# A different start for the first 128 columns of some low weight parts in a two-layer decoder trunk

## The chip, the core and the metric

The kernel runs on one core of a Trainium2 chip. The metric is device time in microseconds (us), from one launch to its end. Three timed runs of the kernel before the change took 2015.96, 2016.24 and 2016.65 us; the median is 2016.24 us.

The core's engines work side by side: TensorE (PE) multiplies matrices, and its weight loads (PEld) are recorded apart; VectorE (DVE) does elementwise work, ScalarE (ACT) copies and activation functions, GpSimd (POOL) and SyncE (SP) start most of the transfers.

## The reference

Two layers over 256 tokens of width 2048, in float32. Layer 0 has full causal attention over its one block of 256 tokens, layer 1 has sliding-window attention (window 128) with shared keys and values and a sink for each head. Both are followed by a gated feed-forward net of width 5504 with a causal convolution of three taps. After each part there is a residual and a layer norm.

```
def conv_ffn(x, w_up, conv_w, conv_b, w_down):
    h = x @ w_up                       # 2048 -> 2 * 5504
    ...                                # causal depthwise convolution, width 3
    g, v = jnp.split(hc, 2, axis=-1)
    return (jax.nn.gelu(g) * v) @ w_down

for layer in range(DEPTH):             # DEPTH = 2
    attn = moba_attention(...) if layer < N_A_LAYERS else swa_attention(...)
    h = layer_norm(ALPHA * h + attn, ln_g[layer, 0], ln_b[layer, 0])
    ffn = conv_ffn(h, ffn_w_up[layer], ffn_conv_w[layer], ffn_conv_b[layer], ffn_w_down[layer])
    h = layer_norm(ALPHA * h + ffn, ln_g[layer, 1], ln_b[layer, 1])
```

Nearly all the time goes into products of 256 tokens with large weight matrices, which are each read once from memory.

## The kernel before

**Two parts for each number.** The multiplier works on a rounded form of float32 (`F32R`). To keep accuracy, each weight `raw` is split into a high part `wh` (a rounded copy, made by ACT, L194) and a low part `wl` = `raw` - `wh` (made by DVE, L203). The activations are split in the same way: `xT` holds, for each of 16 blocks of 128 features, 256 columns of high parts and behind them 256 columns of low parts. A product is the sum of high weight times high activation, high weight times low activation, and low weight times high activation.

**Halves.** Weights stream through in pieces of 128 x 1024 floats, called halves here (`HW = 1024`). Half `s` is loaded by SP into one of 7 `raw` buffers, then split into one of 4 `wh` and one of 4 `wl` buffers. `split_upto` keeps the splits some halves ahead of the use; after each low part it issues the next load.

**Where weights stand still.** In the products for queries, keys and the feed-forward up-projection, a block of 128 x 128 weights is loaded into the multiplier (PEld) and the activations move past it. One unit is 128 output features: two halves, 16 blocks of weights. For each block `k` there is one *high matmul* (weights from `wh`, all 512 columns of `xT[:, k]`: L364, L391) and one *low matmul* (weights from `wl`, the 256 high columns: L367, L391). In the row `L391 PE MATMUL acc<-xT,wl`, `acc` is the accumulator, `xT` the moving operand and `wl` the weights. High matmuls that follow each other are called a high row here, low matmuls that follow each other a low row.

- `ws_unit` (all 52 units of queries and keys, and units 4 to 11 of each up-projection): 8 high, 16 low, 8 high matmuls. Matmuls of attention may be put in after the first half, which cuts the 16 low ones into 8 and 8, or after the second.
- `ws_turns` (units 12 to 85 of each up-projection): 16 high then 16 low in even units, 16 low then 16 high in odd ones. Across units this makes high rows and low rows of 32.
- `ws_opening` (units 0 to 3 of each up-projection): the high matmuls of four units in two passes of 256 columns each (L413), then the low matmuls of the four units (L425) as one row of 64. Units 0 and 1 have `wl` buffers; units 2 and 3 lie in other tiles (`up` in the trace).

In all other products (values, output and down projections) the activations stand still and the weights move.

**The shift.** A `wl` buffer is 64 floats longer than a half (`PAD = 64`). For halves whose weights stand still, the low part is written 48 floats (192 bytes) behind the buffer's first byte (`SHIFT = 48`); for all others, and for halves that lie in other tiles, it starts at the first byte. `wh` always starts at the first byte. In the built program `xT` and all `wh` and `wl` buffers start at the same remainder of 256 bytes, and a block of 128 floats is 512 bytes, so an address differs in this remainder from the others only by the shift.

**Order.** The order on each engine is written out by hand. `next_halves` makes the list of halves with their shifts; `high_upto` takes the buffers; `low_piece` writes the low part; `cols(w, j)` gives the j-th block of 128 columns of a half to a matmul. In the up-projection DVE also does the convolution (L1323 to L1334), and SP and POOL start transfers between places in device memory that sum weights for later (`t<-in_wq_dram`, `t<-t`).

Of the kernel before, what the change touches and what calls it, by code (L numbers as in the profile page):

```python
# [12 lines left out]
F32 = mybir.dt.float32  # L13
F32R = mybir.dt.float32r
AF = mybir.ActivationFunctionType
ALU = mybir.AluOpType
AX = mybir.AxisListType

P = 128
T = 256  # L20
D = 2048
# [4 lines left out]
DFF = 5504  # L26
# [16 lines left out]
HW = 1024  # L43
SHIFT = 48
PAD = 64
# [9 lines left out]
OPENING = 4  # L55
TURNS = 12
# [25 lines left out]
def quad_halves(l, n):  # L82

    if n >= 2:
        return wo_halves(QUADS[l][n])
    q = QUADS[l][n]
    plain = [(k, c) for c in range(2) for k in range(2 * q, FT)]  # L90
    two = lambda *b: ("w", *b, *(plain.pop(0) for _ in range(2 - len(b))))
    order = [two() for _ in range(LEAD[l][n])]
    tight = max(q - (len(plain) - (n * 2 * (DOWN_WINDOW[l] + TRAIL[l]) or 6)) // 2, 0)
    for i, j in enumerate(j for j in TWO_QUADS[l][n] if 2 * j < q):
        for x in range(2):
            a, b = (4 * j + 2 * x, 0), (4 * j + 2 * x + 1, 0)
            sums = [("t", j, 2 * x), ("t", j, 2 * x + 1)]
            if i < tight - (0 if x else q // 2):
                order += [sums[0], two(a, b), sums[1]]
            else:  # L100
                order += [sums[0], two(a), sums[1], two(b)]
        order.append(two((4 * j + 1, 1), (4 * j + 3, 1)))
    return order + [two() for _ in range(len(plain) // 2)]


def wo_halves(q):


    halves = lambda bs: [("w", *bs[i:i + 2]) for i in range(0, len(bs), 2)]
    if q == 6:  # L110
        order = halves([(2 * p + 1, c) for c in range(2) for p in range(q)] + [(12, 0), (13, 0)])
        for i, j in enumerate((2, 0, 1)):
            t = [("t", j, x) for x in range(4)]
            order += t[:2] + halves([(4 * j, 0), (4 * j + 2, 0)]) + t[2:] + (halves(WO_MID) if i == 0 else [])
        return order + halves(WO_LAST)
    q = range(q)
    mid = [b for p in q for b in ((2 * p, 0), (2 * p + 1, 0), (2 * p + 1, 1))]
    mid[5:5] = WO_MID[:1]
    mid[10:10] = WO_MID[1:]
    order = halves(WO_LEAD)  # L120
    sums, others = [("t", j, i) for j in range(len(q) // 2) for i in range(4)], halves(mid)
    while sums:
        order += [sums.pop(0)] + others[:1]
        others = others[1:]
    return order + others + halves(WO_LAST)
# [7 lines left out]
def trunk(ctx: ExitStack, tc: tile.TileContext, wst, wq, xT_in, x_in, relb, umask, sinks, conv_in, ln_g, ln_b, out):  # L133
    nc = tc.nc
# [5 lines left out]
    spool = ctx.enter_context(tc.tile_pool(name="spool", bufs=HALF_BUFS))  # L140
# [4 lines left out]
    tsum = {q: dram.tile([4, P, HW], F32, name=f"t{i}") for i, q in enumerate(QUAD_LIST)}  # L145
    source, used = [], iter(range(wst.shape[0]))

    def next_halves(width, shift=0):
        return [(wst[next(used)], shift) for _ in range(width * D // (P * HW))]

    def next_quads(l, n):
        return [(tsum[l, n, h[1]][h[2]] if h[0] == "t" else wst[next(used)], 0) for h in quad_halves(l, n)]

    for l, width in enumerate((D, KVH * P)):
        if QUADS[l][3]:
            source += next_halves(D // 2) + next_halves(D, SHIFT) + next_quads(l, 3) + next_halves(D, SHIFT)
        else:
            source += next_halves(width) + next_halves((2 * D, KVH * P + D)[l], SHIFT)
        source += next_quads(l, 2) + next_halves(D // 2) if QUADS[l][2] else next_halves(D)
        source += next_halves(2 * DFF, SHIFT) + next_quads(l, 0) + next_quads(l, 1)  # L160
    source, shifts = zip(*source)
    n_halves = len(source)
    raws, halves, aside = {}, {}, {}
# [3 lines left out]
    def pieces(u):  # L167
        return (slice(0, HW // 2), slice(HW // 2, HW)) if u < RAW_FIRST else (slice(0, HW),)
# [11 lines left out]
    def home(tile, j):  # L180

        return [tile[:, k:k + 2, :].rearrange("p a b -> p (a b)") for k in (4 * j, 4 * j + 2)]

    def high_upto(i, behind=None):
        while todo["high"] <= min(i, n_halves - 1):
            s = todo["high"]
            if s in aside:
                wh, wl = home(*aside.pop(s))
            else:
                wh = spool.tile([P, HW], F32R, name="wh")  # L190
                wl = spool.tile([P, HW + PAD], F32R, name="wl")[:, shifts[s]:shifts[s] + HW]
            halves[s] = placed[s] = (wh, wl)
            for j, c in enumerate(pieces(s)):
                nc.scalar.activation(wh[:, c], raws[s][:, c], AF.Copy)  # L194
                if len(pieces(s)) > 1:
                    low_piece(s, c)
                if behind:
                    behind(j)
            todo["high"] += 1

    def low_piece(s, c):
        wh, wl = placed[s]
        nc.vector.tensor_tensor(out=wl[:, c], in0=raws[s][:, c], in1=wh[:, c].bitcast(F32), op=ALU.subtract)  # L203

    def split_upto(i, behind=None):
        while todo["low"] <= min(i, n_halves - 1):
            s = todo["low"]
            high_upto(s, behind)
            if len(pieces(s)) == 1:
                low_piece(s, slice(0, HW))  # L210
            placed.pop(s)
            raws.pop(s)
            load_weights()
            todo["low"] += 1
# [28 lines left out]
    def take(ahead=AHEAD):  # L243
        i = nexth["i"]
        nexth["i"] += 1
        run(ahead_of_splits)
        if i in reach:
            run(before)
        upto = max(i + ahead, reach.get(i, 0))
        if between_splits:  # L250
            high_upto(upto)
            between_splits.pop()()
        split_upto(upto)
        run(before)
        return halves.pop(i)
# [49 lines left out]
    for i, (name, w) in enumerate((("nm", 2), ("rsm", 2), ("sm", 2), ("es", 2), ("ag", 2), ("sd", 1), ("rs", 1))):  # L305
        o = 8 * i - 4 * (name == "rs")
# [46 lines left out]
        nc.vector.scalar_tensor_tensor(b, b, 1 / SCALE, mask.to_broadcast([P, h1 - h0, 2 * P]), op0=ALU.mult, op1=ALU.add)  # L353

    def cols(w, j):
        return w[:, j * P:(j + 1) * P]

    def ws_unit(acc):


        o = acc[:, 0:T]

        def high(wh, k, j, stop=False):
            nc.tensor.matmul(acc, cols(wh, j), xT[:, k, :], start=(k == 0), stop=stop)  # L364

        def low(wl, k, j):
            nc.tensor.matmul(o, cols(wl, j), xT[:, k, 0:T], start=False, stop=False)  # L367

        wh, wl = take()
        for j in range(8):  # L370
            high(wh, j, j)
        for j in range(8):
            low(wl, j, j)
        step()
        wh, wl = take()
        for j in range(8):
            low(wl, 8 + j, j)
        for j in range(8):
            high(wh, 8 + j, j, stop=(j == 7))
        step()  # L380

    def ws_turns(acc, low_first):


        i = nexth["i"]
        pair = [take(AHEAD - 1), take(AHEAD - 2)]

        def row(n, first):
            o, moving = (acc[:, 0:T], slice(0, T)) if n else (acc, slice(0, 2 * T))
            for k in range(KB):  # L390
                nc.tensor.matmul(o, cols(pair[k // 8][n], k % 8), xT[:, k, moving], start=(first and k == 0),  # L391
                                 stop=(not first and k == KB - 1), skip_group_check=True)

        row(int(low_first), True)
        step()
        split_upto(i + 1 + AHEAD)
        run(before)
        row(int(not low_first), False)
        step()
# [224 lines left out]
    def project_out(src, nk, li, homes, preload, turnover=None, work=None, early_sums=None, wo_sums=None, src_pair=None, last_place=None, row_place=None, up=None, direct=None, held=()):  # L624
# [227 lines left out]
        def late(t, i):  # L852
# [15 lines left out]
            if t == 1 and after:  # L868
                first = 3 if work is None else window - 4
                if first <= i < first + 4:  # L870
                    c = COLS[0][i - first]
                    low(0, c, turn(0, c))
                if 5 <= i < 7:
                    high_upto(n0 + i + 1)
# [662 lines left out]
```

## Time and profile before

| | |
|---|---|
| median of three runs | 2016.24 us (2015.96 to 2016.65) |
| the profiled execution | 2015.96 us |
| span from its first to its last instruction | 2014.0 us |
| layer 0: attention with its output projection | up to about 372 us |
| layer 0: up-projection, then down-projection | about 372 to 855, then to 1110 us |
| layer 1: attention with its output projection | up to about 1310 us |
| layer 1: up-projection, then down-projection | about 1310 to 1791, then to 2014 us |

In rows of the timeline the columns are: start, time from the start of the first to the end of the last instruction, engine, line, operation, names, shapes, count. Matmuls are pipelined, and the end that is recorded for one lies beyond the start of the next. So the pace of a row is read from start to start: the start of the next row less the start of this one, divided by the count; or, inside one row, the time of the row less the recorded duration of one matmul, divided by the count less one.

### The profile page before, as it was taken

Reading aid. Unit: us, or ns where it says so; the run is one execution under the profiler, and the core shown is the slowest. Engines: PE = TensorE matmul, PEld = TensorE weight load, DVE = VectorE, ACT = ScalarE, POOL = GpSimd, SP = SyncE. Lnnn points to the kernel's source line nnn. Section 1 sums busy time; section 2 is a strip of 40 time slices with the busy share of each in tenths; the row PEclk is TensorE's granted clock in tenths of the full one; section 3 lists DMA queues with packets and bytes.
Section 4 is the critical chain, followed back from the end, with each engine's and each line's share of the span. In section 5 each row is a group of like instructions: output and inputs, shape, how many; then the busy total and the mean of one; then the engine's idle time right before and its main releaser. Section 6 shows DMA issues by size and latency. Waiting matters only on the chain.

```text
span 2014.0 us, 30061 instructions
## 1 busy us (share of the span) xinstructions
PE 2005.6 (100%) x10894; PEld 1740.1 (86%) x10894; DVE 1699.2 (84%) x2573; ACT 1151.8 (57%) x1648; POOL 130.7 (6%) x177
## 2 busy tenths in 40 slices
PE   9999999999999999999999999999999999999998
PEld 8888888988888888888888888898888888888886
DVE  6878789798888888799997788988888887889988
ACT  5557566345455544477774678545445454467674
POOL 0000000011011010000001000010100011000000
PEclk9999999999999999999999999999999999999999
DMA  9999989899999999589998979989999999769895
GB/s 364 315 265 323 359 257 346 277 329 348 319 333 341 318 345 313 196 301 371 346 396 244 294 240 294 362 239 347 321 323 315 322 324 328 247 197 365 330 366 213
DMA packets 149172, 626.07 MB, mean 311 GB/s; under 512 B 19902, under 2 KB 21310, under 8 KB 136288
## 3 DMA queue, kind: packets, MB, share of 16 engines
q1 hardware_dynamic: 135312, 539.44, 70.7%
q0 software_dynamic: 13424, 84.47, 21.5%
q8 instruction: 85, 1.39, 0.3%
q14 instruction: 63, 0.52, 0.1%
q10 hardware_dynamic: 288, 0.26, 0.0%
HBM read 621.95 MB, written 165.71 MB: 391 GB/s over the span
## 4 chain that ended last, share of the span: by engine, by line
PE 98%; DVE 1%; DMA 0%; ACT 0%; issue 0%; ACTq 0%; DVEq 0%
PE acc L391 41%; PE acc L364 12%; PE acc L367 6%; PE acc L607 5%; PE acc L606 5%; PE acc L605 5%; PE at L607 3%; PE at L606 3%; PE at L605 3%; PE acc L1109 2%; PE acc L450 2%; PE acc L449 2%; PE acc L448 2%; PE acc L413 2%; PE at L967 1%; PE acc L425 1%
## 5 line engine op out<-in xcount | busy, mean ns | idle before, releaser
L203 DVE TENSOR_TENSOR wl<-raw,wh 128x1024 fp32r<-128x1024 f32 (+1 forms) x782 | 944.3, 1215 | 185.8 <-ACT wh L194 112.1
L194 ACT ACTIVATE wh<-raw 128x1024 fp32r<-128x1024 f32 (+1 forms) x782 | 821.8, 1053 | 432.5 <-issue 207.6
L391 PE MATMUL acc<-xT,wh 128*128 128x512 f32 x2368 | 552.5, 391 | 0.0
L391 PEld LDWEIGHTS acc<-xT,wh 128*128 128x128 f32 x2368 | 439.4, 188 | 89.9
L391 PEld LDWEIGHTS acc<-xT,wl 128*128 128x128 f32 x2368 | 289.3, 188 | 5.6
L391 PE MATMUL acc<-xT,wl 128*128 128x256 f32 x2368 | 290.8, 280 | 0.0
L364 PE MATMUL acc<-xT,wh 128*128 128x512 f32 x1088 | 261.6, 392 | 0.0
L364 PEld LDWEIGHTS acc<-xT,wh 128*128 128x128 f32 x1088 | 199.5, 188 | 39.9
L1322 ACT ACTIVATE work<-acc 128x256 f32<-128x256 f32 x172 | 65.6, 382 | 186.0 <-PE acc L391 177.7
L367 PEld LDWEIGHTS acc<-xT,wl 128*128 128x128 f32 x1088 | 139.5, 188 | 5.2
L367 PE MATMUL acc<-xT,wl 128*128 128x256 f32 x1088 | 143.6, 280 | 0.0
L324 POOL DMA_DIRECT2D t<-in_wq_dram x78 | 61.7, 791 | 940.3 <-DMA t<-in_wq_dram 931.1
L324 POOL DMA_DIRECT2D t<-t x78 | 61.0, 781 | 603.6 <-DMA t<-in_wq_dram 422.1
L1325 DVE SCALAR_TENSOR_TENSOR work<-work,cw,work 128x255 f32<-128x255 f32 x172 | 83.2, 484 | 6.1
L1326 DVE SCALAR_TENSOR_TENSOR work<-work,cw,work 128x254 f32<-128x254 f32 x172 | 83.1, 483 | 6.2
L607 PE MATMUL acc<-wh,up 128*128 128x512 f32 x202 | 78.7, 390 | 0.0
L605 PE MATMUL acc<-wh,up 128*128 128x512 f32 x200 | 77.9, 389 | 0.0
L606 PE MATMUL acc<-wl,up 128*128 128x512 f32 x200 | 77.9, 389 | 0.0
L1324 DVE TENSOR_SCALAR work<-work,cw 128x256 f32<-128x256 f32 x172 | 71.3, 415 | 6.2
L1323 DVE TENSOR_TENSOR work<-acc,work 128x256 f32<-128x256 f32 x172 | 72.0, 419 | 2.8 <-ACT work L1322 2.8
L235 ACT ACTIVATE work<-work 128x256 f32<-128x256 f32 x86 | 34.6, 402 | 24.2 <-DVE work L1326 24.0
L607 PEld LDWEIGHTS acc<-wh,up 128*128 128x128 f32 x202 | 37.9, 188 | 7.8
(324 smaller groups left out, 2608.5 us busy)
## 6 DMA issues: line engine op xcount, KB each, us to landing
raw<-in_wst_dram SPq DMA_DIRECT2D x680, 512.0 KB, 6.5
t<-in_wq_dram SPq DMA_DIRECT2D x156, 512.0 KB, 8.4
raw<-t SPq DMA_DIRECT2D x156, 512.0 KB, 5.3
t<-in_wq_dram POOLq DMA_DIRECT2D x78, 512.0 KB, 8.4
t<-t POOLq DMA_DIRECT2D x78, 512.0 KB, 8.0
gb<-in_ln_g_dram SPq DMA_DIRECT2D x16, 256.0 KB, 7.2
gb<-in_ln_b_dram SPq DMA_DIRECT2D x16, 256.0 KB, 7.8
raw<-in_wst_dram SPq DMA_DIRECT2D x10, 256.0 KB, 4.6
```

The source lines that it names most:

```text
L194: nc.scalar.activation(wh[:, c], raws[s][:, c], AF.Copy)
L203: nc.vector.tensor_tensor(out=wl[:, c], in0=raws[s][:, c], in1=wh[:, c].bitcast(F32), op=ALU.subtract)
L324: nc.gpsimd.dma_start(o, a, accum_op=ALU.add, max_dma_last_dim=8 * HW)
L364: nc.tensor.matmul(acc, cols(wh, j), xT[:, k, :], start=(k == 0), stop=stop)
L367: nc.tensor.matmul(o, cols(wl, j), xT[:, k, 0:T], start=False, stop=False)
L391: nc.tensor.matmul(o, cols(pair[k // 8][n], k % 8), xT[:, k, moving], start=(first and k == 0), stop=(not first and k == KB - 1), skip_gro ...
L605: nc.tensor.matmul(bank(key), a[0], wh[:, c], start=key not in begun, stop=False)
L606: nc.tensor.matmul(bank(key), a[0], wl[:, c], start=False, stop=False)
L607: nc.tensor.matmul(bank(key), a[1], wh[:, c], start=False, stop=stop)
L1323: nc.vector.tensor_tensor(out=h, in0=acc[:, 0:T], in1=h, op=ALU.add)
L1325: nc.vector.scalar_tensor_tensor(c[:, 1:T], h[:, 0:T - 1], w[:, 1:2], c[:, 1:T], op0=ALU.mult, op1=ALU.add)
L1326: nc.vector.scalar_tensor_tensor(c[:, 2:T], h[:, 0:T - 2], w[:, 0:1], c[:, 2:T], op0=ALU.mult, op1=ALU.add)
```

## The change

For some halves with a shift, called leading here, `wl` becomes a list of two views of the same buffer: the first 128 columns at the buffer's first byte, and the other 896 where they were, 48 floats further on than without a shift. `cols` picks the view. The first block of such a half is then loaded from the place that it would have without a shift; blocks 1 to 7 are loaded from where they were.

A half leads if a low row begins with it: the first half of each unit of queries and keys (52), and in each up-projection half 0, the first half of units 4 to 11, and the first half of the even units from 12 on (1 + 8 + 37). That is 144 of 841 halves. DVE writes a leading low part in two instructions, of 128 and of 896 columns.

```
-    def next_halves(width, shift=0):
-        return [(wst[next(used)], shift) for _ in range(width * D // (P * HW))]
+    def next_halves(width, shift=0, leads=lambda i: i % 2 == 0):
+        return [(wst[next(used)], (shift, shift > 0 and leads(i))) for i in range(width * D // (P * HW))]
+
+    def leads_up(i):
+
+        return i % 2 == 0 and (i == 0 or i >= 2 * OPENING) and (i < 2 * TURNS or i % 4 == 0)
...
-        source += next_halves(2 * DFF, SHIFT) + next_quads(l, 0) + next_quads(l, 1)
+        source += next_halves(2 * DFF, SHIFT, leads_up) + next_quads(l, 0) + next_quads(l, 1)
...
-                wl = spool.tile([P, HW + PAD], F32R, name="wl")[:, shifts[s]:shifts[s] + HW]
+                wl = spool.tile([P, HW + PAD], F32R, name="wl")
+                shift, leads = shifts[s]
+                wl = [wl[:, 0:P], wl[:, shift + P:shift + HW]] if leads else wl[:, shift:shift + HW]
...
     def low_piece(s, c):
         wh, wl = placed[s]
-        nc.vector.tensor_tensor(out=wl[:, c], in0=raws[s][:, c], in1=wh[:, c].bitcast(F32), op=ALU.subtract)
+        if isinstance(wl, list):
+            spans = ((wl[0], slice(0, P)), (wl[1], slice(P, HW)))
+        else:
+            spans = ((wl[:, c], c),)
+        for o, c in spans:
+            nc.vector.tensor_tensor(out=o, in0=raws[s][:, c], in1=wh[:, c].bitcast(F32), op=ALU.subtract)
...
     def cols(w, j):
+        if isinstance(w, list):
+            return w[1][:, (j - 1) * P:j * P] if j else w[0]
         return w[:, j * P:(j + 1) * P]
```

On PE nothing changes its place. The rows below are the last high half and the low row of units 12 and 13 of the up-projection in layer 0 (in brackets the engines whose semaphores an instruction waits for). Before:

```order
L391 MATMUL acc<-xT,wh 128x512 [waits Activation_49]
L391 MATMUL acc<-xT,wh 128x512 x7
L391 MATMUL acc<-xT,wl 128x256 [waits DVE_49]
L391 MATMUL acc<-xT,wl 128x256 x7
L391 MATMUL acc<-xT,wl 128x256 [waits DVE_49]
```

And of the change, where line 391 has become line 404:

```order
L404 MATMUL acc<-xT,wh 128x512 [waits Activation_49]
L404 MATMUL acc<-xT,wh 128x512 x7
L404 MATMUL acc<-xT,wl 128x256 [waits DVE_49] x2
L404 MATMUL acc<-xT,wl 128x256 x6
L404 MATMUL acc<-xT,wl 128x256 [waits DVE_49]
```

The second low matmul of a leading half now waits for DVE as well, since its weights are written by a second instruction.

On DVE the write of a leading half becomes two. The rows below are from the same up-projection, units 13 and 14 (`work` and `gb` belong to the convolution and to sums). Before:

```order
L1329 TENSOR_TENSOR work_3362<-work_3362,work_3363 128x256
L203 TENSOR_TENSOR wl<-raw,wh 128x1024 x2
L1334 TENSOR_TENSOR st<-work_3362,st 128x256
L509 TENSOR_TENSOR gb_4163<-work_3362 128x256
L499 TENSOR_TENSOR gb_4163<-gb_4163,work_3362 128x128
L512 TENSOR_TENSOR gb_4163<-work_3362,gb_4163 128x128
```

And of the change, where line 203 has become line 214:

```order
L1342 TENSOR_TENSOR work_3394<-work_3394,work_3395 128x256
L214 TENSOR_TENSOR wl<-raw,wh 128x1024
L214 TENSOR_TENSOR wl<-raw,wh 128x128
L214 TENSOR_TENSOR wl<-raw,wh 128x896
L1347 TENSOR_TENSOR st<-work_3394,st 128x256
L522 TENSOR_TENSOR gb_4199<-work_3394 128x256
L512 TENSOR_TENSOR gb_4199<-gb_4199,work_3394 128x128
```

One write of 1024 columns has become one of 128 and one of 896; what stands around it is the same.

More of the change, by code (lines that the diff above doesn't have):

```diff
@@ L146, in trunk @@
     source, used = [], iter(range(wst.shape[0]))
-    def next_halves(width, shift=0):
-        return [(wst[next(used)], shift) for _ in range(width * D // (P * HW))]
+    def next_halves(width, shift=0, leads=lambda i: i % 2 == 0):
+        return [(wst[next(used)], (shift, shift > 0 and leads(i))) for i in range(width * D // (P * HW))]
+    def leads_up(i):
+        return i % 2 == 0 and (i == 0 or i >= 2 * OPENING) and (i < 2 * TURNS or i % 4 == 0)
     def next_quads(l, n):
-        return [(tsum[l, n, h[1]][h[2]] if h[0] == "t" else wst[next(used)], 0) for h in quad_halves(l, n)]
+        return [(tsum[l, n, h[1]][h[2]] if h[0] == "t" else wst[next(used)], (0, False)) for h in quad_halves(l, n)]
     for l, width in enumerate((D, KVH * P)):
```

## The prediction

> **What bounds the kernel now.** I read the page first, then the timeline row by row. The page:
>
> ```profile
> span 2014.0 us, 30061 instructions
> PE 2005.6 (100%) x10894; PEld 1740.1 (86%) x10894; DVE 1699.2 (84%) x2573; ACT 1151.8 (57%) x1648; POOL 130.7 (6%) x177
> PE 98%; DVE 1%; DMA 0%; ACT 0%; issue 0%; ACTq 0%; DVEq 0%
> L391 PE MATMUL acc<-xT,wl 128*128 128x256 f32 x2368 | 290.8, 280 | 0.0
> L367 PE MATMUL acc<-xT,wl 128*128 128x256 f32 x1088 | 143.6, 280 | 0.0
> ```
>
> PE carries 98% of the chain that ended last with no idle time before the low matmuls. So the kernel is as fast as its matmuls follow each other, and the question is the pace of the rows. Two high rows and the low row between them in the up-projection, and the steady end of the first high row in a window of its own:
>
> ```profile
> 495.42 7.46 PE L391 MATMUL acc<-xT,wh 128*128 128x512 f32 x32
> 502.72 3.93 PE L391 MATMUL acc<-xT,wl 128*128 128x256 f32 x32
> 506.48 7.46 PE L391 MATMUL acc<-xT,wh 128*128 128x512 f32 x32
> ...
> 497.96 4.70 PE L391 MATMUL acc<-xT,wh 128*128 128x512 f32 x20
> ```
>
> The low row takes 506.48 - 502.72 = 3.76 us, **117.6 ns a step**. A matmul of the high row lasts 0.39, so the steady high pace is (4.70 - 0.39) / 19 = 226.8 ns, call it 226.7. At that pace 32 steps are 7.25 us, but the row takes 7.30: its first steps lose about 0.05.
>
> Is 117.6 the pace of a low matmul? Here is the end of the opening, its low matmuls, with the first unit behind it:
>
> ```profile
> 391.68 3.79 PE L425 MATMUL acc<-xT,wl 128*128 128x256 f32 x32
> 395.30 4.00 PE L425 MATMUL acc<-xT,up 128*128 128x256 f32 x32
> 399.14 1.09 PE L364 MATMUL acc<-xT,wh 128*128 128x512 f32 x4
> ```
>
> All 64 are low matmuls of the same shape. The first 32 have shifted weights (`wl`) and take 3.62 us, **113.2 ns a step**; the next 32 have unshifted ones (`up`) and take 3.84, **120.0**. So the pace depends on where weights lie, and shifted rows have two paces, 113.2 here and 117.6 in `ws_turns`. Queries and keys show both:
>
> ```profile
> 50.68 2.05 PE L367 MATMUL acc<-xT,wl 128*128 128x256 f32 x16
> 52.57 3.85 PE L364 MATMUL acc<-xT,wh 128*128 128x512 f32 x16
> 56.26 2.05 PE L367 MATMUL acc<-xT,wl 128*128 128x256 f32 x16
> ...
> 61.83 1.10 PE L367 MATMUL acc<-xT,wl 128*128 128x256 f32 x8
> 62.77 0.38 PE L971 MATMUL at<-kT,qT 128*128 128x128 f32 x2
> 62.91 0.60 PE L967 MATMUL at<-kTs,qTs 128*128 128x256 f32 x3
> 63.34 1.10 PE L367 MATMUL acc<-xT,wl 128*128 128x256 f32 x8
> 64.29 3.80 PE L364 MATMUL acc<-xT,wh 128*128 128x512 f32 x16
> ...
> 87.48 0.60 PE L967 MATMUL at<-kTs,qTs 128*128 128x256 f32 x3
> 87.92 1.07 PE L367 MATMUL acc<-xT,wl 128*128 128x256 f32 x8
> 88.83 3.81 PE L364 MATMUL acc<-xT,wh 128*128 128x512 f32 x16
> 92.48 1.69 PE L367 MATMUL acc<-xT,wl 128*128 128x256 f32 x13
> ...
> 1216.91 1.10 PE L367 MATMUL acc<-xT,wl 128*128 128x256 f32 x8
> ...
> 1376.61 2.05 PE L367 MATMUL acc<-xT,wl 128*128 128x256 f32 x16
> ```
>
> Behind a high row, 16 low steps take 1.89 us (118 each) and 8 take 0.94. Behind matmuls of attention, 8 steps at 63.34 take 0.95, but at 87.92 they take 0.91 (113). The instructions and the shift are the same; only what ran ahead differs. I take from this that **a low row keeps the rhythm in which it is entered**, slow or fast, and that all low rows behind a high row of 512 columns are slow.
>
> **What sets the rhythm.** The paces fit one grid. With 6.67 ns as the unit, 226.7 is 34 units, 113.3 is 17 and 120.0 is 18; 117.6 is none (17.6). A fast low row thus stands on the same grid as a steady high row, and the slow one does not. The loads say where the entry is spoilt:
>
> ```profile
> 602.09 3.95 PEld L391 LDWEIGHTS acc<-xT,wl 128*128 128x128 f32 x32
> 602.32 3.93 PE L391 MATMUL acc<-xT,wl 128*128 128x256 f32 x32
> ```
>
> The loads of a low row begin 0.23 us, one high step, ahead of its matmuls: the first low block is loaded while the last high matmul runs. Before, that one load is shifted and the high row's other loads are not. After, it is unshifted, so the last high step is like all the others, and the low row starts on the high row's grid. From there a shifted load beside a 256-column matmul on the grid is what the 113.2 rows are made of. This is an inference: no row shows a low row entered in this way. I choose it over "no effect", because in the opening the pace follows the loads at the very step where they change (391.68 and 395.30).
>
> **The sum, against the profiled execution (2015.96 us: span 2014.0 and 1.96 around it).**
>
> - Low rows of `ws_turns`: 2368 matmuls in rows of 32 are 74 rows. Each goes from 3.76 to 3.62 us: 74 x 0.14 = 10.4.
> - Low rows of 16 in `ws_unit`, 39 of them (the first at 50.68, the last at 1376.61): 16 x 113.2 = 1.81 instead of 1.89, in finer figures 0.07: 39 x 0.07 = 2.7.
> - Low rows of 8 that attention cuts off, 29 of them (the first at 61.83, the last at 1216.91): 8 x 113.2 = 0.906 instead of 0.94: 29 x 0.034 = 1.0. The 8 steps behind attention open with no leading half and keep whatever they find.
> - High rows behind a low row. Behind the slow row at 50.68, 16 high steps take 3.69 us; behind the fast one at 87.92, 3.65. That is 0.04 for each of 39, 1.5. In `ws_turns` a high row of 32 loses 0.05 now (7.30 against 7.25); behind a fast row it should lose what the row at 88.83 does, 3.65 - 16 x 0.2267 = 0.02 to 0.03: 74 x 0.02 = 1.5.
>
> Together 17.1. Against it stands one cost on PE, the last high step, which no longer comes up to 1 ns short: 142 x 1 ns, 0.1. **17.0 us** leave 1999.0 for the profiled execution; the median lies 0.28 higher: 1999.2.
>
> **What the change costs elsewhere.** DVE writes 144 leading parts in two instructions:
>
> ```profile
> L203 DVE TENSOR_TENSOR wl<-raw,wh 128x1024 fp32r<-128x1024 f32 x772 | 937.5, 1222 | 181.2 <-ACT wh L194 107.7 <-issue 49.1 <-PE acc L391 1.3
> L499 DVE TENSOR_TENSOR qTs<-qT,qTs 128x128 fp32r<-128x128 f32 x32 | 9.4, 293 | 1.1
> ...
> 445.00:600.00 155.00, 155.00 (x898) 136.94 (x897) 131.81 (x219) 77.20 (x114) 16.36 (x21) 1.00 1.01 331
> ```
>
> From 128 to 1024 columns a subtraction grows by 929 ns, 1.037 a column, so 896 columns take about 1089 and the pair 1382, 160 more than one: 144 x 0.16 = 23 us of DVE. In the window 445 to 600 DVE is busy 131.81 of 155 us (the third pair of figures); the 14 leading halves there add 2.2 to 23 idle. In the view of waits PE waits for four things in the whole span, and no low part is among them. If that cover were gone, the 23 us would stand on PE's path; I take nothing, with 1 us for the range. The second wait, on the second low matmul, costs nothing while DVE is ahead: rows of 32 hold waits at matmuls 1, 9, 17 and 25 now, and keep their pace. In the opening the row is fast already; if the new entry made it slow it would cost 2 x 32 x 4.4 ns = 0.3 us.
>
> What is late next is the supply. The same row has the DMA engines busy all the time (share 1.01, the last but one figure) at 331 GB/s, and the up-projections would be 1.5% shorter. In 445 to 857 no engine waits for `raw`; over the whole span it is:
>
> ```profile
> ACT wh L194 <- DMA raw<-in_wst_dram: 24.7, 28, 2.8
> ```
>
> I take nothing here, and up to 8 us given back as a rival. Behind attention, 8-step rows may change rhythm with the new entry: between 10 rows lost (+0.6, with their high rows) and 19 gained (-1.2).
>
> **A rule that speaks against the change.** In the Trainium skill, "SBUF — State Buffer", section "Who interferes with whom", gives PE two independent read ports, one for the moving operand and one for weight loads; by it where weights lie changes nothing, the low rows stay as they are, and the time is 2016. The trace does not agree: 113.2 and 120.0 ns in one row of 64. In the Trainium skill, "TensorE: Matmul & The Clock Gate", section "Back-to-back issue gap", gives 256 columns 109.2 ns (256/2.4 + 2.5); by it 3224 low matmuls would have an estimated 27 us to gain, but no low row here is faster than 113.
>
> **The rivals.**
>
> 1. *No effect* (0.10). The row starts on the grid, but the first shifted load throws it into the slow rhythm, as in the row at 63.34, which the same attention matmuls precede as the fast one at 87.92. For it: I can't say from rows why one of these two is slow. The independent ports would give the same. DVE's 23 us are hidden: 2016.2, within 0.5.
> 2. *Slower: the unshifted rhythm sticks* (0.06). The row opens with an unshifted load and runs on at 120.0, as the row at 395.30 does, if the first step decides for the whole row. The rows concerned hold 2368 + 39 x 16 + 29 x 8 = 3224 low matmuls: 3224 x 2.4 ns = 7.7 us, 2023.9. Against it: at 395.30 the pace changes where the loads do, not where the row was entered.
> 3. *Faster, but given back* (0.08). Either the supply eats up to half the gain (2000 to 2008), or only one of the two kinds of row turns fast: `ws_turns` alone is 10.4 + 1.5, 2004.3; `ws_unit` alone is 5.2, 2011.0.
>
> **How the numbers follow.** The forecast, all leading rows fast, has 0.76: 1999.2, and by the bounds above (high rows gain nothing, 3.0 less; attention rows between +0.6 and -1.2; DVE 1) between 1997 and 2004. I take the range 1997 to 2008, which takes in most of rival 3 and leaves out no effect, slower and `ws_unit` alone, together under 0.2. Under 0.2% either way (4 us) a measurement of this kernel can hardly tell from no change. Faster by more than that: 0.76 and 0.08, 0.84. Within it: 0.10. Slower: 0.06.
>
> **What would show it.** Right: low rows of 32 take 3.62 us from start to start, the recorded low matmul of `ws_turns` falls from 280 to 276 ns as in L425, a high row of 32 takes 7.28, and DVE shows 144 more instructions and some 23 us more. Wrong: low rows at 3.76 (rival 1) or 3.84 (rival 2) with PE still at 100%; or low rows at 3.62 with PE idle, ACT waiting for `raw` in the up-projections or PE for `wl` (rival 3).

## The result and the profile after

The changed kernel takes 1999.67 us (median of 6 runs, 1998.93 to 2001.02) against 2016.10 for the kernel before beside it (6 runs, 2015.96 to 2016.65). The ratio is 0.9918, with a 95% interval of 0.9905 to 0.9931: 0.8% faster. The forecast was 1999.2.

The page of the changed kernel, in the order of the lines shown of before. Behind the bar stand busy time, mean ns of one, and idle time before them:

```profile
span 1997.7 us, 30210 instructions
PE 1989.6 (100%) x10894; PEld 1727.1 (86%) x10894; DVE 1708.0 (85%) x2717; ACT 1150.9 (58%) x1648; POOL 130.9 (7%) x177
PE 98%; DVE 1%; DMA 0%; issue 0%; ACT 0%; ACTq 0%; POOL 0%; POOLq 0%; DVEq 0%
L404 PE MATMUL acc<-xT,wl 128*128 128x256 f32 x2368 | 280.5, 276 | 0.0
L380 PE MATMUL acc<-xT,wl 128*128 128x256 f32 x1088 | 139.9, 277 | 0.0
```

PE still carries 98% of the chain, without idle time before the low matmuls. The number of matmuls is the same, and the recorded low one fell from 280 to 276 ns. The span is 16.3 us shorter. The timeline shows where. First the up-projection, a high row, a low row and a high row; then the first units of queries and keys (columns as before: start, time of the row, engine, line, names, shapes, count):

```profile
492.51 7.44 PE L404 MATMUL acc<-xT,wh 128*128 128x512 f32 x32
499.80 3.79 PE L404 MATMUL acc<-xT,wl 128*128 128x256 f32 x32
503.42 7.44 PE L404 MATMUL acc<-xT,wh 128*128 128x512 f32 x32
510.70 0.50 PE L404 MATMUL acc<-xT,wl 128*128 128x256 f32 x3
...
49.57 1.98 PE L377 MATMUL acc<-xT,wh 128*128 128x512 f32 x8
51.38 1.98 PE L380 MATMUL acc<-xT,wl 128*128 128x256 f32 x16
53.20 3.81 PE L377 MATMUL acc<-xT,wh 128*128 128x512 f32 x16
56.85 1.98 PE L380 MATMUL acc<-xT,wl 128*128 128x256 f32 x16
```

Low rows of 32 take 3.62 us from start to start (3.76 before), high rows behind them 7.28 or 7.29 (7.30), low rows of 16 take 1.81 or 1.82 (1.89), and high rows of 16 take 3.65 (3.69). Added up start to start over every matmul of the two traces, the low matmuls of `ws_turns` (L391, now L404) save 10.43 us and those of `ws_unit` (L367, now L380) 3.71; the high ones save 1.43 and 1.52. Together that is 17.1 us. The span shows 0.8 less. Most of it is lost ahead of everything that the change touches: the first row of `ws_unit` starts at 49.57 us, before it was 48.87. Repeated starts of the same work differ by as much (49.67 us with the split alone, below, and 48.79 with leading parts in all halves), so this belongs to the execution that was profiled, not to the change.

DVE, by form, and one leading half in the timeline:

```profile
L214 DVE TENSOR_TENSOR wl<-raw,wh 128x896 fp32r<-128x896 f32 x144 | 156.2, 1085 | 0.1
L214 DVE TENSOR_TENSOR wl<-raw,wh 128x128 fp32r<-128x128 f32 x144 | 41.7, 290 | 52.7 <-issue 46.0 <-ACT wh L200 6.7
...
446.43 1.29 DVE L214 TENSOR_TENSOR wl<-raw,wh 128x128 fp32r<-128x128 f32 x2 [0.67 <-issue]
```

The two writes of a leading half last 290 and 1085 ns, but from the start of the first to the end of the second it is 1.29 us, since their recorded times overlap. DVE's busy time grew by 8.8 us (1699.2 to 1708.0), and in the view of waits no instruction of PE waits for a low part.

### The profile page after: what moved, and what is told of

Read it like the earlier page. It is cut to its first block, busy times and chain, and to the rows that moved or that the text cites. A ratio compares the mean times of both kernels' runs of the same rounds, so it can differ in the third digit from the quotient of the medians.

```text
span 1997.7 us, 30210 instructions
## 1 busy us (share of the span) xinstructions
PE 1989.6 (100%) x10894; PEld 1727.1 (86%) x10894; DVE 1708.0 (85%) x2717; ACT 1150.9 (58%) x1648; POOL 130.9 (7%) x177
## 4 chain that ended last, share of the span: by engine, by line
PE 98%; DVE 1%; DMA 0%; issue 0%; ACT 0%; ACTq 0%; POOL 0%; POOLq 0%; DVEq 0%
PE acc L404 40%; PE acc L377 12%; PE acc L380 6%; PE acc L618 5%; PE acc L620 5%; PE acc L619 5%; PE at L618 4%; PE at L620 4%; PE at L619 4%; PE acc L1122 2%; PE acc L463 2%; PE acc L461 2%; PE acc L462 2%; PE acc L426 2%; PE at L980 1%; PE acc L438 1%
## 5 line engine op out<-in xcount | busy, mean ns | idle before, releaser
L214 DVE TENSOR_TENSOR wl<-raw,wh 128x1024 fp32r<-128x1024 f32 (+3 forms) x926 | 953.7, 1050 | 171.9 <-ACT wh L200 101.3
L404 PE MATMUL acc<-xT,wh 128*128 128x512 f32 x2368 | 551.1, 390 | 0.0
L404 PEld LDWEIGHTS acc<-xT,wh 128*128 128x128 f32 x2368 | 439.3, 188 | 88.2
L404 PEld LDWEIGHTS acc<-xT,wl 128*128 128x128 f32 x2368 | 279.4, 188 | 5.7
L404 PE MATMUL acc<-xT,wl 128*128 128x256 f32 x2368 | 280.5, 276 | 0.0
L380 PEld LDWEIGHTS acc<-xT,wl 128*128 128x128 f32 x1088 | 136.3, 188 | 5.3
L380 PE MATMUL acc<-xT,wl 128*128 128x256 f32 x1088 | 139.9, 277 | 0.0
```

Of the source, the lines that this page charges most:

```text
L214: nc.vector.tensor_tensor(out=o, in0=raws[s][:, c], in1=wh[:, c].bitcast(F32), op=ALU.subtract)
```

## The experiments

The theory, for rows of shifted weights: the pace of a low row is set by how it is entered; it is fast if the load beside the last high matmul has the remainder of 256 bytes of the other loads in the high row. In the rows below, a low row of 32 at 3.62 us is fast and one at 3.76 slow. Where steps of single matmuls are given, they are read from start to start in the trace. The kernel before ran beside each group of kernels: 2016.52 us beside the split without the move, `ws_turns` alone, the place at 128 bytes and the leading block in every half; 2016.63 beside the place at 256 bytes, no shift, shifted high parts and the first run of leading high halves; 2016.88 beside the last four.

**The split without the move.** Line 197 of the changed kernel:

```
-                wl = [wl[:, 0:P], wl[:, shift + P:shift + HW]] if leads else wl[:, shift:shift + HW]
+                wl = [wl[:, shift:shift + P], wl[:, shift + P:shift + HW]] if leads else wl[:, shift:shift + HW]
```

> As the changed kernel, but the first 128 columns of a leading half stay 48 floats in, where they were: only the second DVE write and the second wait are left. Theory (the place of that one load sets the rhythm of the row): low rows of 32 stay at 3.76 us from start to start, the recorded low matmul of the up-projection at 280 ns, time 2016.1 within 1. Rival (an extra wait or an earlier write lets the row start in time): rows of 32 fall to 3.62 us, 276 ns, time near 1999.7. DVE's extra work, about 22 us, should cost nothing in either.

Measured: 2016.86 us, ratio 1.000 (0.9991 to 1.001). A low row of the up-projection in its timeline, to the start of the next high row:

```profile
503.65 3.93 PE L404 MATMUL acc<-xT,wl 128*128 128x256 f32 x32
507.42 1.78 PE L404 MATMUL acc<-xT,wh 128*128 128x512 f32 x7
```

3.77 us: slow. The second write and the second wait cost nothing that can be measured and bring nothing. The whole gain is the place of one block in a half.

**Leading halves in `ws_turns` alone.**

```
-    def next_halves(width, shift=0, leads=lambda i: i % 2 == 0):
+    def next_halves(width, shift=0, leads=lambda i: False):
...
-        return i % 2 == 0 and (i == 0 or i >= 2 * OPENING) and (i < 2 * TURNS or i % 4 == 0)
+        return i >= 2 * TURNS and i % 4 == 0
```

> As the changed kernel, but only the even units from 12 on of the up-projections lead (74 halves); queries, keys, the opening and units 4 to 11 are as before. Theory: the 74 low rows of 32 take 3.62 us and the high rows behind them 7.28; the rows of 16 and 8 keep 118 ns a step. Gain 10.4 + 1.4 = 11.8, time 2004.3 within 1. Rival (the gain comes in part from what is ahead of the up-projection, such as earlier transfers): a gain that differs from 11.8 by over 1.5.

Measured: 2004.86 us, ratio 0.9939 (0.9925 to 0.9954), 11.7 us below the kernel before beside it. A unit of queries and keys, and a row of the up-projection, in its timeline:

```profile
51.24 2.05 PE L380 MATMUL acc<-xT,wl 128*128 128x256 f32 x16
53.12 3.85 PE L377 MATMUL acc<-xT,wh 128*128 128x512 f32 x16
...
502.53 3.79 PE L404 MATMUL acc<-xT,wl 128*128 128x256 f32 x32
506.15 5.18 PE L404 MATMUL acc<-xT,wh 128*128 128x512 f32 x22
```

Rows that lead are fast (3.62 us), the others stay slow (1.88 for 16). Added up start to start, L404 saves 10.42 and 1.42 us, the same as in the full change: what is gained in one place does not depend on the other.

**The leading block at another wrong place.**

```
-                wl = [wl[:, 0:P], wl[:, shift + P:shift + HW]] if leads else wl[:, shift:shift + HW]
+                wl = [wl[:, 32:32 + P], wl[:, shift + P:shift + HW]] if leads else wl[:, shift:shift + HW]
```

> As the changed kernel, but the first 128 columns of a leading half lie 32 floats (128 bytes) behind the buffer's first byte, not at it. Theory (only a load at the remainder of the high row's loads keeps the last high step at 34 units of 6.67 ns): the row is entered off the grid and low rows of 32 stay at 3.76 us; high rows behind them at 7.30; time 2014 to 2017. Rival (any start apart from the 48 floats will do, since it is the change of place within the row that matters): 3.62 us and 1999.7.

Measured: 2018.16 us, ratio 1.0007 (0.9998 to 1.0017). In its timeline:

```profile
497.36 7.49 PE L404 MATMUL acc<-xT,wh 128*128 128x512 f32 x32
504.69 3.94 PE L404 MATMUL acc<-xT,wl 128*128 128x256 f32 x32
508.46 7.49 PE L404 MATMUL acc<-xT,wh 128*128 128x512 f32 x32
```

The low row takes 3.77 us, slow as expected. The high row takes 7.32 matmul by matmul, 0.02 more than before, which was not expected. Over the high rows of `ws_turns` that is 1.7 us, and the time lies past the range. Its last step, beside the load that is off, takes 233 ns where it took 226. The rest is lost in its first steps, behind the slow low row (the first takes 241 ns where it took 235); why these are longer, no run shows.

**The leading block 256 bytes further on.** The buffer is 64 floats longer, and both views move by 64 floats (`PAD = 128`, descriptor area 3072 bytes):

```
-                wl = [wl[:, 0:P], wl[:, shift + P:shift + HW]] if leads else wl[:, shift:shift + HW]
+                wl = [wl[:, 64:64 + P], wl[:, 64 + shift + P:64 + shift + HW]] if leads else wl[:, shift:shift + HW]
```

> As the changed kernel, but the first 128 columns of a leading half lie 64 floats (256 bytes) behind the buffer's first byte, the other 896 a further 64 floats on as well, so that both remainders of 256 bytes are as in the changed kernel; buffers are 64 floats longer, and the area for transfer descriptors is 3072 in place of 4096 bytes to make room. Theory (only the remainder of 256 bytes counts): rows of 32 at 3.62 us, time 1999.7 within 1. Rival (what counts is the buffer's first byte itself or a longer period): rows of 32 at 3.7 to 3.8, 2014 or more.

Measured: 1999.63 us, ratio 0.9914 (0.9898 to 0.9931).

```profile
492.19 7.44 PE L404 MATMUL acc<-xT,wh 128*128 128x512 f32 x32
499.48 3.79 PE L404 MATMUL acc<-xT,wl 128*128 128x256 f32 x32
503.10 2.23 PE L404 MATMUL acc<-xT,wh 128*128 128x512 f32 x9
```

3.62 us, as in the changed kernel. The first byte of the buffer is nothing special: a leading block at 0 or 256 bytes does the same, one at 128 or 192 does not. A leading block at 64 bytes was not tried.

**No shift at all.** In the kernel before, `SHIFT = 48` becomes `SHIFT = 0`.

> The kernel before with no shift at all: every low part starts at its buffer's first byte. Theory (with loads and rows on one remainder every low matmul takes 18 units of 6.67 ns, and nothing ever leaves the grid): low rows of 32 take 3.84 us, 120.0 a step, and high rows behind them lose about 0.02 us, as behind the unshifted end of the opening. 3456 low matmuls less the fast ones of before x 2.2 to 6.7 ns is 7.6 us slower, high rows 2.9 us faster: 2021 within 2. Rival (the shift matters only through the entry of rows): 3.62 to 3.76 us a row and a time of 2000 to 2016.

Measured: 2021.19 us, ratio 1.0023 (1.0014 to 1.0033).

```profile
503.69 4.00 PE L391 MATMUL acc<-xT,wl 128*128 128x256 f32 x32
507.52 7.44 PE L391 MATMUL acc<-xT,wh 128*128 128x512 f32 x32
514.80 1.48 PE L391 MATMUL acc<-xT,wl 128*128 128x256 f32 x11
```

The low row takes 3.83 us, 120 ns a step, and the high row behind it 7.28 in place of 7.30, both as expected. The entry is that of the changed kernel, and the first step of the row takes 113 ns as there; the other 31 take 120. So a good entry alone does not make a row fast: the blocks behind the first must be shifted too. The shift earns 4.6 us in the kernel before, and 21.5 once rows are entered in time (2021.19 against 1999.7).

**A leading block in every half.**

```
-    def next_halves(width, shift=0, leads=lambda i: i % 2 == 0):
+    def next_halves(width, shift=0, leads=lambda i: True):
...
-        return i % 2 == 0 and (i == 0 or i >= 2 * OPENING) and (i < 2 * TURNS or i % 4 == 0)
+        return True
```

> As the changed kernel, but the first 128 columns of every half with a shift lie at the buffer's first byte, so that a low row of 32 has an unshifted load ahead of its matmuls 1, 9, 17 and 25. Theory (an unshifted load beside a low matmul makes that step 18 units of 6.67 ns in place of 17, which leaves the grid as it is): a row of 32 takes 3.62 + 3 x 0.0067 = 3.64 us, of 16 0.007 more than in the changed kernel; sum 74 x 0.020 + 39 x 0.007 = 1.8 us slower than the changed kernel, 2001.5, and rows behind attention may turn fast (up to 1.2 less). Rival (one load off its place throws the row out of its rhythm for good): from the second half of a row on the pace is 117.6 or 120, a row of 32 takes 3.72 to 3.78, time 2010 to 2019.

Measured: 2007.41 us, ratio 0.9955 (0.9940 to 0.9969), 7.7 us slower than the changed kernel where the theory said 1.8. A low row of 32 and the high row behind it, and then, from views of that row by line in two windows, the recorded time of its matmuls (count, then least, median and largest ns, then the first and last start):

```profile
499.91 3.89 PE L404 MATMUL acc<-xT,wl 128*128 128x256 f32 x32
503.64 7.43 PE L404 MATMUL acc<-xT,wh 128*128 128x512 f32 x32
510.90 0.28 PE L404 MATMUL acc<-xT,wl 128*128 128x256 f32 x1
...
L404 PE MATMUL acc<-xT,wl x7: 276/276/276, 499.9 to 500.6; 128*128 128x256 f32 x7
...
L404 PE MATMUL acc<-xT,wl x20: 277/279/280, 501.1 to 503.3; 128*128 128x256 f32 x20
```

The row takes 3.73 us. Its first matmuls are those of a fast row, 276 ns; behind the second half's unshifted block they are those of a slow one, 279. From start to start, eight steps take 113 or 114 ns, the ninth 121, and the rest 117 to 119 (115 at the end of each later half). The rival was right on this: one block off its place inside a low row throws the row out for the rest of its length. Its time was not: 2007.41 lies below its 2010 to 2019 as it lies above the theory's 2001.5. The theory gave an unshifted load inside a fast row one step of 18 units and no effect on the steps behind it; that is refuted. The theory holds for the entry from a high row, not for any single load. The high row behind takes 7.26 us, less than the 7.28 of the changed kernel, though its low row is slow; no run explains this.

**High parts shifted as well.** In the kernel before, `wh` of halves whose weights stand still is also written 48 floats in:

```
-                wh = spool.tile([P, HW], F32R, name="wh")
+                wh = spool.tile([P, HW + PAD], F32R, name="wh")[:, shifts[s]:shifts[s] + HW]
```

> The kernel before, but high parts whose weights stand still are shifted by 48 floats like the low ones, so that no load in high or low rows changes its remainder, and both differ from that of the activations (descriptor area 3072 bytes). Theory as far as it goes (the place of weights against the activations sets the pace, and a row keeps the grid it is entered on): low rows of 32 at 3.62 us (10.4 and 3.7 us less), and high steps at 226.7 or, if the shift saves them a unit as it does in low rows, at 220.0 (3456 x 6.7 ns = 23 us less): 2002 or 1979. Rival (the slow rhythm belongs to shifted loads beside matmuls of 512 columns): high steps off the grid, low rows at 3.76, 2016 or slower.

Measured: 2011.25 us, ratio 0.9973 (0.9963 to 0.9983), which is none of the times expected (2002, 1979, 2016 or more). Two low rows with the high rows behind them, and the inside of one high row:

```profile
490.37 3.93 PE L391 MATMUL acc<-xT,wl 128*128 128x256 f32 x32
494.14 7.49 PE L391 MATMUL acc<-xT,wh 128*128 128x512 f32 x32
501.46 3.79 PE L391 MATMUL acc<-xT,wl 128*128 128x256 f32 x32
505.09 7.48 PE L391 MATMUL acc<-xT,wh 128*128 128x512 f32 x32
...
495.74 4.97 PE L391 MATMUL acc<-xT,wh 128*128 128x512 f32 x21
```

High steps now take (4.97 - 0.39) / 20 = 229 ns, 34.3 of the units of 6.67 ns: the high row is off the grid, as the rival said. The low rows behind it are slow (3.77 us) or fast (3.63), by turns (38 and 36 of the 74) and with no load that changes its remainder in between. So neither side had it right, and the theory as it is put above is not enough: the load beside the last high matmul has the remainder of all others here, and half the low rows are slow. It fits that the rhythm of the row ahead decides, and not the remainder as such: weights and activations lie at the same places in all these rows, and there are two paces in one stage. It is not shown, because the accumulators do not lie at the same place: four take turns (`bufs=4`), and a low row of 32 uses two of them, so that they alternate with the rows. In the kernel before and in the changed one the same turns of accumulators go with one pace; their place was not varied alone.

**High rows entered in time, too.** The changed kernel with the same idea turned round (the new list of views for `wh` is used in the writes and in `cols` as that of `wl` is):

```
+    def highs_up(i):
+        return i % 4 == 2 if i >= 2 * TURNS else i >= 2 * OPENING and i % 2 == 1
...
+                wh = [wh[:, shift:shift + P], wh[:, PAD + P:PAD + HW]] if highs else wh[:, 0:HW]
```

> The changed kernel, and the same idea turned round for high rows: where a high row follows a low row, the first 128 columns of the high part are shifted by 48 floats, so that the load beside the last low matmul is like the others of that row (74 - 2 x 1 halves in the up-projections from unit 12 on, 16 in units 4 to 11, 52 in queries and keys; ACT writes these high parts in two instructions, DVE takes the differences in two; descriptor area 3072 bytes). Theory: the last low step stays at 113.3 ns, the high row starts on the grid and loses nothing: a high row of 32 takes 7.253 in place of 7.280 us, of 16 3.627 in place of 3.654. Sum 113 x 0.027 = 3.0 us faster than the changed kernel, 1996.7. Rival (the jump from a shifted to an unshifted load, one step later, costs the same and throws the high row off in the same way): 7.28 us and 1999.7.

Measured: 1996.86 us, ratio 0.9903 (0.9888 to 0.9918).

```profile
498.78 3.79 PE L416 MATMUL acc<-xT,wl 128*128 128x256 f32 x32
502.40 7.42 PE L416 MATMUL acc<-xT,wh 128*128 128x512 f32 x32
509.66 1.52 PE L416 MATMUL acc<-xT,wl 128*128 128x256 f32 x12
```

The high row takes 7.26 us, and loses nothing. To compare the two on one chip, both ran again in one group:

> The changed kernel again, beside the runs below on one chip: 1999.7 within 0.7; low rows of 32 at 3.62 us.

> The kernel with leading low and high halves again: 3.0 us faster than the changed kernel beside it if its gain is that of the rows (high rows of 32 at 7.253 us); by the rival (its gain was luck of the runs) the two agree within 1 us.

Measured: 1999.83 us (1999.41 to 2000.63; ratio 0.9916, 0.9901 to 0.9931) and 1996.82 (1996.27 to 1997.66; ratio 0.9902, 0.9885 to 0.9919). The difference is 3.0 us, as worked out from the rows; the first run of this version, 1996.86, lay 2.8 us below the 1999.63 of the place at 256 bytes, which ran beside it and has the rows of the changed kernel. The intervals of the two ratios overlap, but the highest run of the one in this group lies below the lowest of the other, and the rows carry the whole difference. This version is faster than both kernels.

**Other shifts,** in that version, `SHIFT = 32` and `SHIFT = 16`:

> The kernel with leading low and high halves, with a shift of 32 in place of 48 floats. Theory (the shift sets the pace of a row that is entered in step; 48 gives 17 units): another pace of a whole number of units or off the grid, to be read; if 17 units are the floor of a low matmul, 3.62 us a row of 32 or more and no time below 1996. Rival (the floor is lower): rows of 32 at 3.41 us (16 units), 23 us less.

> The same with a shift of 16 floats. Theory and rival as for 32: 3.62 us a row of 32 or more, or 3.41.

Measured: 2017.41 and 1996.91 us. A low row of each, with the high row before or behind it:

```profile
503.19 3.95 PE L416 MATMUL acc<-xT,wl 128*128 128x256 f32 x32
506.98 7.45 PE L416 MATMUL acc<-xT,wh 128*128 128x512 f32 x32
...
498.97 3.79 PE L416 MATMUL acc<-xT,wl 128*128 128x256 f32 x32
502.59 2.66 PE L416 MATMUL acc<-xT,wh 128*128 128x512 f32 x11
```

With 32 floats the row takes 3.79 us, 118.4 ns a step, which is 17.8 units and off the grid; with 16 floats 3.62, the same as with 48. The two are not the same everywhere. In the opening, where the low row is entered from high matmuls of 256 columns, the 32 low matmuls with `wl` weights are slow with 16 floats and fast with 48 (first the opening of this run, then that of the version with 48 floats):

```profile
389.79 3.93 PE L450 MATMUL acc<-xT,wl 128*128 128x256 f32 x32
393.55 2.68 PE L450 MATMUL acc<-xT,up 128*128 128x256 f32 x21
...
389.53 3.80 PE L450 MATMUL acc<-xT,wl 128*128 128x256 f32 x32
393.17 3.04 PE L450 MATMUL acc<-xT,up 128*128 128x256 f32 x24
```

They take 3.76 and 3.64 us. No shift that was run gave a low matmul below 113.3 ns, so nothing speaks for the 16 units of the rival.

## Why the prediction was right

- **The bound and the cover.** PE set the time before and after. The split alone took nothing measurable, so DVE's two writes and the second wait stayed hidden. Their size was overestimated: 23 us of DVE were worked out from durations, 0.16 a pair, and the busy time grew by 8.8. Recorded times of neighbours on DVE overlap: the pair above takes 1.29 us from start to end, 0.07 more than one write. The term stood outside the sum, so this did not touch the forecast.
- **The inference.** No row of before showed a low row entered behind an unshifted load beside a 512-column matmul. The prediction chose this mechanism with 0.76 and said that it was inferred; the runs bear it out. The case with the split alone shows that the place of this block is the cause, and the places at 128 and 256 bytes show that its remainder of 256 bytes is what counts. The last high step, about 1 ns shorter than the others before, is like them now, as the prediction said, and the low steps of `ws_turns` went from 117.7 to 113.3 ns. Why a load at another remainder shifts the rhythm was not tried.
- **The terms.** Low rows of 32: 10.4 forecast, 10.43 found. Rows of 16 and 8: 2.7 + 1.0 forecast, 3.71 found. High rows: 1.5 + 1.5 forecast, 1.52 + 1.43 found. The 1 ns per last high step was right to leave at 0.1. Together 17.1 us were found in the rows, and 17.0 were forecast. The median fell by 16.4 in the first comparison and by 17.05 in the last.
- **Rows behind attention.** They were left at nothing, between +0.6 and -1.2. Ten of 29 were fast before, ten are fast after, but not all the same ones. That the balance is nothing is luck: the prediction could not say which rows would turn, and no run says why one is slow and another fast.
- **The supply.** The window 445 to 600, with 339 GB/s after 331 and a DMA share of 1.02 after 1.01, moved the shorter up-projection's weights without a wait on PE; from 445 to 857 us no engine waits for `raw`, as before:

```profile
445.00:600.00 155.00, 155.00 (x917) 137.16 (x916) 134.33 (x235) 77.29 (x114) 17.27 (x22) 1.00 1.02 339
```

- **The rivals.** No effect is what the load at 128 bytes and the split alone give; a pace of 120.0 in a row of 32 was seen only where every block of it was unshifted (the kernel without a shift, and the second half of the opening), never after one unshifted block. The rule of the Trainium skill ("SBUF — State Buffer", section "Who interferes with whom") that the two read ports are independent, from which the prediction read that the place of weights changes nothing, does not give these times: the same matmuls take 113.3, 117.6 or 120.0 ns by the place of weights alone. The 27 us that the prediction estimates from 109.2 ns a low matmul were out of reach: 113.3 is the best of any run here.
- **What does not carry further.** The prediction counts in whole units of 6.67 ns on one grid. Taken beyond the change, this failed twice: with a leading block in every half (2007.4 us against 2001.5) and with shifted high parts, whose high rows are off the grid (2011.25 against 2002 or 1979). The grid describes the steady high rows, the fast rows and the unshifted rows of this kernel; it is not shown to be a rule.

## What to carry to other kernels

When the same matmul has two recorded durations in one trace (276 and 280 ns here), compare what runs ahead of the two kinds of rows before looking at the rows themselves: a start-to-start pace over a whole row resolves a nanosecond, and 4.4 ns in 3224 matmuls are 14 us. The place of the one block of weights that is loaded across a change of rows can be worth more than that of all others: here 16.4 us at the change from high to low rows and 3.0 more at the change back, where the shift of all blocks had been worth 4.6. A shift that was chosen while rows were entered out of time should be measured again when they are not: here it was worth 4.6 us and then 21.5.

## What was not expected

- A single unshifted block inside a fast low row makes the rest of it slow: 276 ns up to it, 279 after it, and 3.73 us a row in place of 3.62. At the entry from a high row, an unshifted block makes a row of otherwise shifted ones fast.
- With high and low parts shifted alike, no load changes its remainder, and yet low rows alternate between 3.77 and 3.63 us. The high rows between them are off the grid (229 ns a step); that this is the reason was not tried apart from the accumulators, which alternate too.
- Behind 512-column high rows, shifts of 64 and 192 bytes give the same fast row (3.62 us), one of 128 bytes gives 3.79; in the opening 64 bytes are slow and 192 fast. What it is in the memory or the multiplier that makes the unit of 6.67 ns was not settled by any run.
